# One substitution for all four head pairs: the triangular inverse of an RWKV-7 layer, one 32x32 block per partition

## The chip, the cores and the metric

The kernel runs on one core of a Trainium2 chip. The metric is the device time of one execution in microseconds. Line numbers are those of the kernel before the change; lines of the changed kernel stand only in the order and the diff, and are 1 less behind the changed function and 2 less behind the place that calls it.

## What is computed

One decoder layer on 2048 tokens of width 1024: an RMS norm, one wide projection, three branches (RWKV-7 time mixing with 8 heads of 64, sliding-window attention, cross-attention into 256 memory tokens), a projection of each branch under a gate, their sum, and an output projection. The change lies in the RWKV branch, whose state is computed token by token in the reference:

```python
def rwkv7_scan(r, w, k, v, a, b):
    def step(S, inp):
        r_t, w_t, k_t, v_t, a_t, b_t = inp
        sa = jnp.einsum('bhvk,bhk->bhv', S, a_t)
        S = S * w_t[:, :, None, :] + sa[..., None] * b_t[:, :, None, :] + v_t[..., None] * k_t[:, :, None, :]
        y = jnp.einsum('bhvk,bhk->bhv', S, r_t)
        return S, y
...
h = rms_norm(x, norm_g[l])
p = h @ w_in[l]
...
merged = (gates[:, :, 0] * (y_a @ w_proj_a[l]) + gates[:, :, 1] * (y_b @ w_proj_b[l])
          + gates[:, :, 2] * (y_c @ w_proj_c[l]))
x = x + (merged.astype(x.dtype) @ w_out[l]).astype(x.dtype)
```

The kernel computes it in chunks of 64 tokens. Within a chunk the tokens depend on each other through a unit triangular 64x64 matrix per head, and its inverse is needed before the chunk's state can be computed.

## The kernel before

The tokens are worked on in four blocks of 512 (the loop over `sb`). A block has 8 chunks, and the 8 heads are taken as 4 pairs. For a block, two streams of work are written out beside each other. `stream_r` is the RWKV branch: `rwkv_prep` for each pair (projections, decays, the products of a chunk), `rwkv_inverse` for the triangular matrices of two pairs, and once all four pairs are through, `rwkv_chain`, which carries the state through the 8 chunks and ends with the normalised output of each pair. `stream_f` is all the rest: cross-attention heads, the attention pairs, the merges of two branches (`merge`) and the gates. Each stream yields numbers, `paced` multiplies them by the factors of `PACE` (line 38), and `weave` lets the stream with the smaller sum go on. That gives the order in which instructions are written.

From this order a planner in the kernel (`steps` and `lay_out`, called by `order`) makes the final one. It goes through the program with its own costs per instruction and puts down, engine by engine, which ready instruction comes next by its rank; a tile's buffer has to be free first. So a change of the pools, the pacing or one function can move instructions everywhere. Each engine's instructions then stand in this order, and so do the DMAs of each queue: most are issued by SyncE, the loads of x's rows by ScalarE.

Matmuls of the projections are done in float32r with each operand as a high and a low part, so three matmuls of 512 columns per product (`gemm3`, lines 532 to 534). A weight tile `whl` holds both parts of four 128x128 blocks, 4 KB per partition, and serves 12 matmuls. There are `WR` = 7 of them. In the first block the parts are made from the raw weight (`wblock`, ScalarE L513, VectorE L514) and mostly kept in DRAM; later blocks load them (L509). Outputs go through two PSUM buffers named `mm`. The factors of a pair lie in tiles `big`, also 4 KB per partition, `BIG` = 6 of them: QE, QO, AB and BK for a pair in `rwkv_prep`, and Q and B of a chunk in the chain. AB of a pair stays until `rwkv_inverse` has put the inverse into it.

`rwkv_inverse` works on two pairs, 16 matrices of 64x64. Their diagonal 32x32 blocks, 64 of them, are stored to DRAM (`fn`, L843) and loaded so that one partition holds one block (L885). As there are 128 partitions, each block is loaded twice, and partition p and p+64 each compute half of the columns. A forward substitution of 31 steps, a multiply (L890) and an add (L891) on VectorE each, inverts them. The result goes out (L893, `fy`) and comes back with a block's rows on the partitions (L896), is transposed (L899), and two bursts of 32x32 matmuls (L911 and L919, with copies of the first one's output by L914 between) make the off-diagonal blocks. ScalarE puts them into AB (L904, L923), and SyncE stores AB (`put`, L756) to DRAM, from where the chain fetches it chunk by chunk (L942). The call for pairs 0 and 1 stands ahead of `rwkv_prep` of pairs 2 and 3.

At the end of a block the chain's outputs are transposed (L1032), scaled, gated and split into high and low parts (L1062, L1063), and `merge` projects them (L1315 empties the PSUM buffer, L1316 adds). In the middle of this, `x_scales` prepares the next block: it loads rows of x (L1357), ScalarE sums their squares (L1359), VectorE adds the halves (L1361), POOL makes the scale, VectorE spreads it (L570) and TensorE transposes it (L572).

Of the kernel before, what the change touches and what calls it, by code (L numbers as in the profile page):

```python
# [9 lines left out]
F32 = mybir.dt.float32  # L10
# [4 lines left out]
AF = mybir.ActivationFunctionType  # L15
ALU = mybir.AluOpType
# [3 lines left out]
T, D, M = 2048, 1024, 256  # L20
TB = 512
NG = 9
WR = 7
BIG = 6
NRT = 6
AT1, AT2 = 4, 8
SCRATCH = 1024
# [5 lines left out]
NC_ = TB // C  # L33
# [1 line left out]
DEC = 0.5 * math.exp(-0.5)  # L35


PACE = [[[1.2] * 20 + [0.8] * 20, [1.35] * 120] for _ in range(2)]


B_R, B_K, B_V, B_WA, B_ZA, B_Q, B_SK, B_SV, B_ZB, B_XQ, B_ZC, B_G = 0, 4, 8, 12, 13, 17, 21, 22, 23, 27, 31, 35
# [275 lines left out]
def build(tc, A, nsb=4):  # L317
    nc = tc.nc
    es = ExitStack()
    V, S, G, PE = nc.vector, nc.scalar, nc.gpsimd, nc.tensor  # L320
# [8 lines left out]
    rp = pool("rp", 1)  # L329
# [15 lines left out]
    def rw_ps():  # L345
        return ps.tile([128, 512], F32, name="rw", bufs=2)
# [145 lines left out]
    dp = pool("dp", 1, space=bass.MemoryType.DRAM)  # L492
# [382 lines left out]
    def rwkv_inverse(group, parks, fn, fy):  # L875

        n = len(group) * NC_
        halves = [(slice(b, b + 32), slice(b + 32, b + 64)) for b in (0, 64)]
        Nb = rp.tile([128, 32, 32], F32, name="km", bufs=2)
        B = rp.tile([128, 16, 32], F32, name="Yi")  # L880
        flat = B.rearrange("p a t -> p (a t)")
        G.memset(flat, 0.0)
        for j in range(2):
            own = slice(64 * j, 64 * j + 64)
            nc.sync.dma_start(Nb[own], fn.rearrange("q i c s t -> (q i c) s t"))  # L885
            G.memset(flat[own, j:j + 511:34], 1.0)
        for s in range(31):
            w, m = 31 - s, s // 2 + 1
            bc = rp.tile([128, 16, 32], F32, name="ibc", bufs=2)
            V.tensor_tensor(bc[:, :m, :w], Nb[:, s, s + 1:].unsqueeze(1).to_broadcast([128, m, w]), B[:, :m, s:s + 1].to_broadcast([128, m, w]), op=ALU.mult)  # L890
            V.tensor_tensor(B[:, :m, s + 1:], B[:, :m, s + 1:], bc[:, :m, :w], op=ALU.add)  # L891
        for j in range(2):
            nc.sync.dma_start(fy.rearrange("q i c (a j) t -> j (q i c) a t", j=2)[j], B[64 * j:64 * j + 64])  # L893
        Y = rp.tile([128, n, 32], F32, name="Yi")
        for q in range(4):
            nc.sync.dma_start(Y[32 * q:32 * q + 32], fy[q].rearrange("i c s t -> s (i c) t"))  # L896
        yield 27
        X = rp.tile([128, n, 32], F32, name="ibc", bufs=2)
        V.transpose(X.rearrange("p a b -> p (a b)"), Y.rearrange("p a b -> p (a b)"))  # L899
        for i, g in enumerate(group):  # L900
            for q in range(4):
                qs = slice(32 * q, 32 * q + 32)
                to = slice(32 * (q ^ g[0] // 2 * 2), 32 * (q ^ g[0] // 2 * 2) + 32)
                S.activation(g[1][to, :, 32 * (q % 2):32 * (q % 2) + 32], Y[qs, i * NC_:(i + 1) * NC_], AF.Copy)  # L904
        R = rp.tile([128, n, 32], F32, name="ibc", bufs=2)
        pr = rw_ps().rearrange("p (c t) -> p c t", t=32)
        ms = []
        for i, g in enumerate(group):
            for c in range(NC_):
                for u, l in halves:  # L910
                    ms.append(PE.matmul(pr[l, i * NC_ + c], g[1][u, c, 32:64], X[u, i * NC_ + c], start=True, stop=True))  # L911
        together(ms)
        for u, l in halves:
            V.tensor_copy(R[l], pr[l])  # L914
        po = rw_ps().rearrange("p (c t) -> p c t", t=32)
        ms = []
        for c in range(n):
            for u, l in halves:
                ms.append(PE.matmul(po[u, c], R[l, c], Y[l, c], start=True, stop=True))  # L919
        together(ms)  # L920
        for i, g in enumerate(group):
            for (u, l), (to, _) in zip(halves, halves[::-1] if g[0] > 1 else halves):
                S.activation(g[1][to, :, 32:64], po[u, i * NC_:(i + 1) * NC_], AF.Copy)  # L923
        for g in group:
            put(g[1], parks[1], g[0], 0)
        yield 4
# [458 lines left out]
    for i, _ in enumerate(mem_kv(mT)):  # L1385
        if i == AT1:
            rb = x_scales(0)
        if i == AT2:
            masks()
            hT = x_cols(0, rb)  # L1390
    for sb in range(nsb):
        wa = proj(B_WA, hT)
        low = shift(wa, B_WA, pcol("mu_wa"), dcol("omu_wa"), sb, "rr_")
        S.activation(low[EV], low[EV], AF.Tanh)

        lwla = [rp.tile([128, TB], F32R, name=f"lwla{i}") for i in range(2)]
        for t, h, o in zip(lwla, (EV, OD), (OD, EV)):
            S.activation(t[h], low[h], AF.Copy)
            V.tensor_tensor(t[o], low[h], t[h].bitcast(F32), op=ALU.subtract)
        yas = []  # L1400
        ya, yb, yc_ = ([], []), ([], []), ([], [])
        accs = []

        def stream_r():
            parks = park(sb)
            dk = xp.tile([128, 4, NC_], F32, name="dk", bufs=1)
            Pl = xp.tile([128, 4, NC_], F32, name="Pl", bufs=1)
            yts = []
            for p0 in (0, 2):
                group = []  # L1410
                fn, fy = (dp.tile([4, 2, NC_, 32, 32], F32, name=f"{n}{sb}_{p0}") for n in ("fn", "fy"))
                for p in (p0, p0 + 1):
                    yield from rwkv_prep(p, p - p0, parks, dk, Pl, fn, sb, hT, lwla, group)
                yield from rwkv_inverse(group, parks, fn, fy)
                yts += [g[2] for g in group]
            yield from rwkv_chain(parks, dk, Pl, hT, yts, yas)
            yield 0.412

        def stream_f():
            for h in range(4):  # L1420
                yield from cross_head(h, sb, hT, *yc_)
            if not sb:
                rope_tables(0)
            yield from swa_kv(sb, hT)
            yield 6.938
            for j in range(4):
                yield from weave(swa_pair(j, sb, hT, *yb), merge(2, *yc_, accs, hT, first=True, orange=(2 * j, 2 * j + 1)))
            yield from merge(1, *yb, accs, hT)
            for o in range(8):
                gates.append(gate(0, o, hT))  # L1430
                yield 5.908

        gates = []
        for _ in weave(*(paced(g, PACE[min(sb, 1)][i]) for i, g in enumerate((stream_r(), stream_f())))):
            pass
        for p in range(4):
            split_y(yas[p], *ya, "a", p, sb)
        rb = None
        if sb + 1 < nsb:
            rope_tables(sb + 1)  # L1440
            rb = x_scales(sb + 1)
        parts = []
        for o in range(8):
            for _ in merge(0, *ya, accs, hT, gates=gates, orange=(o,)):
                pass
            parts.append(split_acc(accs[o]))
        if rb is not None:
            hT = x_cols(sb + 1, rb)
        output(sb, *zip(*parts))
# [91 lines left out]
```

## Time and profile before

| | |
|---|---|
| three runs | 2147.26 us median, 2144.42 to 2148.93 |
| the profiled execution | 2148.25 us, span 2146.4 us |
| TensorE busy | 2129.0 us, 99% |
| weight loads (PEld) | 1754.6 us, 82% |
| VectorE | 1418.3 us, 66% |
| ScalarE | 805.7 us, 38% |
| DMA | 519.18 MB, 242 GB/s |

A share of the span says how long an engine had something to do. The profile also lists what each engine waited for, the chain of work that ended last, and the instructions in order of time.

### The profile page before, as it was taken

The page shows a single profiled execution, that of the slowest core. Times are in us where ns is not written, and L with a number is a line of the kernel's source. Part 1 is how long each engine was busy: PE and PEld are TensorE (multiplying, and loading weights), DVE is VectorE, ACT ScalarE, POOL GpSimd, SP SyncE. Part 2 cuts the span into 40 slices and gives each one's busy share as a digit, 9 for nine tenths or more (in the row PEclk, how much of TensorE's full clock was granted, in tenths as well). Part 3 has the DMA queues.
Part 4 walks back from the last instruction along what each step waited for, and adds up shares of the span by engine and source line. Part 5 has one row for each costly group of instructions (what it writes and reads, how often), then busy time and mean ns, then how long its engine had stood idle before and what let it go on. Part 6 is the DMA issues. An engine that isn't in the chain of part 4 may idle for free.

```text
span 2146.4 us, 37466 instructions
## 1 busy us (share of the span) xinstructions
PE 2129.0 (99%) x14260; PEld 1754.6 (82%) x14260; DVE 1418.3 (66%) x3234; ACT 805.7 (38%) x1703; POOL 138.5 (6%) x180
## 2 busy tenths in 40 slices
PE   9999999999999999999999999999999999999999
PEld 7888887878888888878788888887878888888787
DVE  7879888568477787455647778736455777873532
ACT  7655554336343343204423434410523334331220
POOL 2101000001001000001000000000100010000000
PEclk9999999999999999999999999999999999999999
DMA  9987888988866677686876657777776666768665
GB/s 337 356 280 266 271 290 282 341 288 269 296 207 193 182 219 229 198 298 207 283 255 207 193 175 224 230 224 261 248 254 217 204 201 200 230 188 268 218 205 182
DMA packets 308595, 519.18 MB, mean 242 GB/s; under 512 B 89280, under 2 KB 175552, under 8 KB 308416
## 3 DMA queue, kind: packets, MB, share of 16 engines
q1 hardware_dynamic: 292288, 487.42, 70.1%
q10 hardware_dynamic: 16128, 29.37, 4.2%
q8 instruction: 113, 1.85, 0.3%
q14 instruction: 66, 0.54, 0.1%
HBM read 378.80 MB, written 137.89 MB: 241 GB/s over the span
## 4 chain that ended last, share of the span: by engine, by line
PE 89%; DMA 4%; DVE 3%; ACT 2%; issue 1%; POOL 0%; SPq 0%; ACTq 0%; DVEq 0%; POOLq 0%
PE mm L532 22%; PE mm L534 22%; PE mm L533 22%; PE mm L1332 1%; PE mm L1334 1%; PE mm L1333 1%; DMA rt<-in_x 1%; PE rw L1014 1%; PE oo L1281 1%; PE rw L997 1%; PE rw L829 1%; PE rw L848 1%; DVE whl L514 1%; PE oo L829 1%; DMA raw<-in_w_in 0%
## 5 line engine op out<-in xcount | busy, mean ns | idle before, releaser
L532 PE MATMUL mm<-hH,whl 128*128 128x512 f32 x1888 | 745.2, 395 | 1.5 <-DVE carry L740 1.4
L533 PE MATMUL mm<-hL,whl 128*128 128x512 f32 x1888 | 743.3, 394 | 0.1
L534 PE MATMUL mm<-hH,whl 128*128 128x512 f32 x1888 | 741.7, 393 | 0.0
L532 PEld LDWEIGHTS mm<-hH,whl 128*128 128x128 f32 x1888 | 354.7, 188 | 73.0 <-ACT whl L513 1.8
L534 PEld LDWEIGHTS mm<-hH,whl 128*128 128x128 f32 x1888 | 354.7, 188 | 71.8
L533 PEld LDWEIGHTS mm<-hL,whl 128*128 128x128 f32 x1888 | 355.0, 188 | 70.4 <-DVE hL L1381 0.6
L513 ACT ACTIVATE whl<-raw 128x512 fp32r<-128x512 f32 x174 | 109.1, 629 | 184.8 <-PE mm L534 135.0
L514 DVE TENSOR_TENSOR whl<-raw,whl 128x512 fp32r<-128x512 f32 x174 | 120.1, 692 | 64.4 <-ACT whl L513 61.4
L532 PE MATMUL mm<-yh,whl 128*128 128x512 f32 x384 | 151.9, 396 | 3.7 <-DVE g L1315 2.1
L534 PE MATMUL mm<-yh,whl 128*128 128x512 f32 x384 | 151.4, 394 | 0.0
L533 PE MATMUL mm<-yl,whl 128*128 128x512 f32 x384 | 150.7, 392 | 0.0
L1300 ACT ACTIVATE gt<-mm 128x512 f32<-128x512 f32 x64 | 37.7, 590 | 178.7 <-PE mm L534 178.7
L532 PEld LDWEIGHTS mm<-yh,whl 128*128 128x128 f32 x384 | 72.5, 189 | 20.8 <-DVE g L1315 2.9
L533 PEld LDWEIGHTS mm<-yl,whl 128*128 128x128 f32 x384 | 72.5, 189 | 15.0 <-DVE yl L1063 0.2
L534 PEld LDWEIGHTS mm<-yh,whl 128*128 128x128 f32 x384 | 72.5, 189 | 15.1
L1315 DVE SCALAR_TENSOR_TENSOR gt<-gt,mm 128x512 f32<-128x512 f32 x32 | 22.0, 687 | 94.3 <-PE mm L534 93.9
L485 POOL TENSOR_SCALAR st<-st 128x4 f32<-128x4 f32 (+1 forms) x32 | 13.2, 413 | 1031.4 <-DVE st L1091 401.4
L1339 DVE SCALAR_TENSOR_TENSOR ya<-mm,ya 128x512 f32<-128x512 f32 x16 | 11.0, 690 | 97.7 <-PE mm L1334 97.7
L1249 ACT ACTIVATE g<-g,mxs,st 128x128 f32<-128x128 f32 x128 | 61.5, 483 | 27.9 <-DVE mxs L1242 27.9
L890 DVE TENSOR_TENSOR ibc<-km,Yi 128x126 f32<-128x126 f32 (+22 forms) x248 | 63.0, 254 | 7.6 <-DMA km<-fn 1.2
L891 DVE TENSOR_TENSOR Yi<-Yi,ibc 128x126 f32<-128x126 f32 (+22 forms) x248 | 62.7, 253 | 5.0
L489 POOL TENSOR_TENSOR st<-st,mhalf 128x8 f32<-128x8 f32 (+1 forms) x36 | 53.7, 1491 | 3.0
(1829 smaller groups left out, 3587.0 us busy)
## 6 DMA issues: line engine op xcount, KB each, us to landing
whl<-k SPq DMA_DIRECT2D x474, 512.0 KB, 4.0
k<-whl SPq DMA_DIRECT2D x162, 512.0 KB, 4.8
raw<-in_w_in SPq DMA_DIRECT2D x118, 256.0 KB, 4.1
fq<-big SPq DMA_DIRECT2D x64, 256.0 KB, 4.3
fb<-big SPq DMA_DIRECT2D x64, 256.0 KB, 4.2
big<-fq SPq DMA_DIRECT2D x32, 512.0 KB, 6.6
big<-fb SPq DMA_DIRECT2D x32, 512.0 KB, 5.6
ya<-in_x ACTq DMA_DIRECT2D x32, 256.0 KB, 4.8
```

The source lines that it names most:

```text
L489: G.tensor_tensor(out, out, mhalf[:, :n], op=ALU.pow)
L513: S.activation(w[:, 0], raw, AF.Copy)
L514: V.tensor_tensor(w[:, 1], raw, w[:, 0].bitcast(F32), op=ALU.subtract)
L532: PE.matmul(out, lh, rh, start=i == 0, stop=False)
L533: PE.matmul(out, lh, rl, start=False, stop=False)
L534: PE.matmul(out, ll, rh, start=False, stop=i == n - 1)
L829: m = PE.matmul(g[:, c], BK[h, c0 + c], Q[h, c0 + c], start=True, stop=True)
L890: V.tensor_tensor(bc[:, :m, :w], Nb[:, s, s + 1:].unsqueeze(1).to_broadcast([128, m, w]), B[:, :m, s:s + 1].to_broadcast([128, m, w]), op= ...
L891: V.tensor_tensor(B[:, :m, s + 1:], B[:, :m, s + 1:], bc[:, :m, :w], op=ALU.add)
L1249: S.activation(P_, P_, AF.Exp, scale=r2[:, b, i:i + 1], bias=mx[:, b, i:i + 1], accum_out=mx[:, b, 2 + i:3 + i])
L1300: S.activation(t, gp, AF.Tanh, scale=0.5)
L1315: V.scalar_tensor_tensor(g, g, 1.0, pp, op0=ALU.add, op1=ALU.mult)
```

## The change

`rwkv_inverse` is called once per block of tokens, behind `rwkv_prep` of all four pairs. It then has 128 diagonal blocks, one for each partition: they are loaded once, a step works on s+1 columns instead of s//2+1, and one store and one load (in four parts) replace two of each. The two bursts of matmuls have 64 instead of 32 matmuls and two PSUM buffers each, and the copies between them are four instead of two. The temporary `ibc` shrinks from 2 KB to 1 KB per partition (two buffers), `Yi` grows from 2 KB to 4 KB, X and R move to the tag `km`. As the ABs of four pairs stay until the inverse is there, `BIG` goes from 6 to 7, and `WR` from 7 to 6, tiles of the same size. The pacing of `stream_r` up to the chain goes from 20 yields at 1.2 to 18 at 1.4, in all four blocks.

```diff
-WR = 7
-BIG = 6
+WR = 6
+BIG = 7
...
-PACE = [[[1.2] * 20 + [0.8] * 20, [1.35] * 120] for _ in range(2)]
+PACE = [[[1.4] * 18 + [0.8] * 20, [1.35] * 120] for _ in range(2)]
...
-        B = rp.tile([128, 16, 32], F32, name="Yi")
+        B = rp.tile([128, 32, 32], F32, name="Yi")
...
-        for j in range(2):
-            own = slice(64 * j, 64 * j + 64)
-            nc.sync.dma_start(Nb[own], fn.rearrange("q i c s t -> (q i c) s t"))
-            G.memset(flat[own, j:j + 511:34], 1.0)
+        nc.sync.dma_start(Nb, fn.rearrange("q i c s t -> (q i c) s t"))
+        G.memset(flat[:, ::33], 1.0)
         for s in range(31):
-            w, m = 31 - s, s // 2 + 1
-            bc = rp.tile([128, 16, 32], F32, name="ibc", bufs=2)
-            V.tensor_tensor(bc[:, :m, :w], Nb[:, s, s + 1:].unsqueeze(1).to_broadcast([128, m, w]), B[:, :m, s:s + 1].to_broadcast([128, m, w]), op=ALU.mult)
-            V.tensor_tensor(B[:, :m, s + 1:], B[:, :m, s + 1:], bc[:, :m, :w], op=ALU.add)
-        for j in range(2):
-            nc.sync.dma_start(fy.rearrange("q i c (a j) t -> j (q i c) a t", j=2)[j], B[64 * j:64 * j + 64])
+            w, m = 31 - s, s + 1
+            bc = rp.tile([128, 256], F32, name="ibc", bufs=2)[:, :m * w].rearrange("p (a t) -> p a t", t=w)
+            V.tensor_tensor(bc, Nb[:, s, s + 1:].unsqueeze(1).to_broadcast([128, m, w]), B[:, :m, s:s + 1].to_broadcast([128, m, w]), op=ALU.mult)
+            V.tensor_tensor(B[:, :m, s + 1:], B[:, :m, s + 1:], bc, op=ALU.add)
+        nc.sync.dma_start(fy.rearrange("q i c s t -> (q i c) s t"), B)
...
-        yield 27
-        X = rp.tile([128, n, 32], F32, name="ibc", bufs=2)
-        V.transpose(X.rearrange("p a b -> p (a b)"), Y.rearrange("p a b -> p (a b)"))
+        yield 30
+        X = rp.tile([128, n, 32], F32, name="km", bufs=2)
+        for b in range(0, n, 16):
+            V.transpose(X[:, b:b + 16].rearrange("p a b -> p (a b)"), Y[:, b:b + 16].rearrange("p a b -> p (a b)"))
...
-        R = rp.tile([128, n, 32], F32, name="ibc", bufs=2)
-        pr = rw_ps().rearrange("p (c t) -> p c t", t=32)
+        R = rp.tile([128, n, 32], F32, name="km", bufs=2)
+        pr = [rw_ps().rearrange("p (c t) -> p c t", t=32) for _ in range(2)]
...
-        for u, l in halves:
-            V.tensor_copy(R[l], pr[l])
-        po = rw_ps().rearrange("p (c t) -> p c t", t=32)
+        for b in range(2):
+            for u, l in halves:
+                V.tensor_copy(R[l, 16 * b:16 * b + 16], pr[b][l])
+        po = [rw_ps().rearrange("p (c t) -> p c t", t=32) for _ in range(2)]
...
-            for p0 in (0, 2):
-                group = []
-                fn, fy = (dp.tile([4, 2, NC_, 32, 32], F32, name=f"{n}{sb}_{p0}") for n in ("fn", "fy"))
-                for p in (p0, p0 + 1):
-                    yield from rwkv_prep(p, p - p0, parks, dk, Pl, fn, sb, hT, lwla, group)
-                yield from rwkv_inverse(group, parks, fn, fy)
-                yts += [g[2] for g in group]
+            group = []
+            fn, fy = (dp.tile([4, 4, NC_, 32, 32], F32, name=f"{n}{sb}") for n in ("fn", "fy"))
+            for p in range(4):
+                yield from rwkv_prep(p, p, parks, dk, Pl, fn, sb, hT, lwla, group)
+            yield from rwkv_inverse(group, parks, fn, fy)
+            yts += [g[2] for g in group]
```

The planner then lays out everything anew. Three places of the new order bear on what follows. In the rows a name like `g_10628` is a buffer with its number.

VectorE at the boundary of the second and third block, where `x_scales` of the third block meets the first output tiles of `merge`. Before:

```order
L614 TENSOR_SCALAR cosT<-rt 128x512
L514 TENSOR_TENSOR whl<-raw,whl 128x512
L1361 TENSOR_TENSOR rs<-ss 128x4
L1315 SCALAR_TENSOR_TENSOR g_10628<-g_10628,mm 128x512
L514 TENSOR_TENSOR whl<-raw,whl 128x512
L1316 TENSOR_TENSOR mB<-mB,g_10628 128x512
L570 COPY rt<-rs 128x512
```

And now:

```order
L614 TENSOR_SCALAR cosT<-rt 128x512
L514 TENSOR_TENSOR whl<-raw,whl 128x512 x2
L1314 SCALAR_TENSOR_TENSOR g_10463<-g_10463,mm 128x512
L1315 TENSOR_TENSOR mB<-mB,g_10463 128x512
L1360 TENSOR_TENSOR rs<-ss 128x4
L1321 TENSOR_TENSOR mB<-mB,g_11001 128x512
L1314 SCALAR_TENSOR_TENSOR g_10558<-g_10558,mm 128x512
```

The instruction that empties the first `mm` buffer (L1315, now L1314) stood behind the sum `rs` and now stands ahead of it; that of the second output tile stays behind it.

SyncE's queue in the second block, the stores of AB (`fb`) behind the second burst and the chain's first fetch of them, among loads of weight tiles. Before:

```order
L756 DMA fb_0_6544<-big 128x4x128
L756 DMA fb_1_6545<-big 128x4x128
L509 DMA whl<-k_5085 128x1024
L509 DMA whl<-k_5092 128x1024
L756 DMA fb_0_6544<-big 128x4x128
L756 DMA fb_1_6545<-big 128x4x128
L509 DMA whl<-k_5140 128x1024
L942 DMA big<-fb_0_6544 128x1024
```

And now, the last five of eight stores and the fetch:

```order
L756 DMA fb_1_6431<-big 128x4x128
L509 DMA whl<-k_4963 128x1024
L756 DMA fb_0_6430<-big 128x4x128
L509 DMA whl<-k_4971 128x1024
L756 DMA fb_1_6431<-big 128x4x128
L509 DMA whl<-k_4978 128x1024
L756 DMA fb_0_6430<-big 128x4x128
L509 DMA whl<-k_5089 128x1024
L756 DMA fb_1_6431<-big 128x4x128
L509 DMA whl<-k_5097 128x1024
L941 DMA big<-fb_0_6430 128x1024
```

There were four stores ahead of the first fetch and are eight, and a weight load stands behind nearly each of them. On TensorE the order has 108 dense matmuls between the second burst and the chain's first use of AB (L1006) where it had 70 (109 and 71 in the first block).

TensorE at the end of the first block, from the last transposes of the chain's output (L1032, now L1031). Rows with `hH` and `hL` are matmuls of a gate, rows with `yh` and `yl` of the projection of that output. Before:

```order
L1032 MATMUL rw<-c_ident,rt 128x128 x4
L534 MATMUL mm<-hH,whl 128x512
L532 MATMUL mm<-hH,whl 128x512
L533 MATMUL mm<-hL,whl 128x512
L534 MATMUL mm<-hH,whl 128x512
L532 MATMUL mm<-hH,whl 128x512
L533 MATMUL mm<-hL,whl 128x512
L534 MATMUL mm<-hH,whl 128x512
L532 MATMUL mm<-hH,whl 128x512
L533 MATMUL mm<-hL,whl 128x512
```

And now:

```order
L1031 MATMUL rw<-c_ident,rt 128x128 x4
L534 MATMUL mm<-hH,whl 128x512
L532 MATMUL mm<-hH,whl 128x512
L533 MATMUL mm<-hL,whl 128x512
L534 MATMUL mm<-hH,whl 128x512
L532 MATMUL mm<-hH,whl 128x512
L533 MATMUL mm<-hL,whl 128x512
L534 MATMUL mm<-hH,whl 128x512
L532 MATMUL mm<-yh,whl 128x512
L533 MATMUL mm<-yl,whl 128x512
```

31 matmuls of gates stood between the last transposes and the projection; 7 do now. Of the projection, 9 matmuls of each of two output tiles come next, which need the first three pairs, and then those of the fourth.

## Rows read from the trace of the kernel before

**Rows 1.** The page, part 1: busy us of each engine, share, instructions.
```profile
PE 2129.0 (99%) x14260; PEld 1754.6 (82%) x14260; DVE 1418.3 (66%) x3234; ACT 805.7 (38%) x1703; POOL 138.5 (6%) x180
```

**Rows 2.** Windows: stretch, its length, each engine's busy us, PEclk, DMA share, GB/s.
```profile
200.00:300.00 100.00, 98.41 (x731) 81.76 (x730) 85.86 (x177) 51.19 (x107) 6.70 (x10) 1.00 0.84 273
...
600.00:700.00 100.00, 100.00 (x539) 83.46 (x538) 70.95 (x158) 39.44 (x85) 8.79 (x10) 1.00 0.67 201
...
1038.00:1042.00 4.00, 4.00 (x14) 3.23 (x13) 2.34 (x4) 1.23 (x2) 0.00 (x0) 0.57 0.97 321
```

**Rows 3.** What TensorE waited for: us in total, times, longest.
```profile
PE mm L532 <- DVE g L1315: 2.1, 1, 2.1
PE mm L532 <- DVE carry L740: 1.4, 1, 1.4
PE as__11203 L572 <- DVE rt L570: 1.2, 1, 1.2
PE mm L532 <- DVE gt L1315: 1.2, 1, 1.2
```

**Rows 4.** Timeline of TensorE around a second burst: start, us, instruction, idle before.
```profile
1282.67 0.39 PE L533 MATMUL mm<-hL,whl 128*128 128x512 f32 x1
1282.99 1.20 PE L919 MATMUL rw<-Yi,ibc 32*32 32x32 f32 x64
1284.12 0.50 PE L765 MATMUL rw<-lwla,whl 128*128 128x512 f32 x1
1284.46 0.40 PE L766 MATMUL rw<-lwla,whl 128*128 128x512 f32 x1
```

**Rows 5.** The substitution's multiply: the page's group, and one shape by form.
```profile
L890 DVE TENSOR_TENSOR ibc<-km,Yi 128x126 f32<-128x126 f32 (+22 forms) x248 | 63.0, 254 | 7.6 <-DMA km<-fn 1.2
...
L890 DVE TENSOR_TENSOR ibc<-km,Yi 128x126 f32<-128x126 f32 x24 | 7.0, 290 | 0.4
```

**Rows 6.** Timeline of TensorE at the boundary of the second and third block.
```profile
1029.45 0.39 PE L532 MATMUL mm<-yh,whl 128*128 128x512 f32 x1
...
1033.30 0.39 PE L534 MATMUL mm<-yh,whl 128*128 128x512 f32 x1
1035.83 0.50 PE L532 MATMUL mm<-yh,whl 128*128 128x512 f32 x1 [2.13 <-DVE g L1315]
...
1037.78 0.75 PE L572 MATMUL as__11203<-c_ident,rt 128*128 128x128 f32 x4 [1.22 <-DVE rt L570]
```

**Rows 7.** The chain that ended last in that stretch: start, us, what.
```profile
1025.95 8.22 DMA rt<-in_x
...
1035.01 0.07 DVE rs L1361
...
1035.09 0.68 DVE g L1315
```

**Rows 8.** SyncE's queue's waits (us, times, longest); landing times of weight tiles.
```profile
SPq L509 <- PE mm L534: 789.7, 352, 7.0
...
SPq L843 <- DVE big L836: 49.0, 14, 7.0
...
DMA to landing us min/median/max: 2.7/4.1/9.9
```

**Rows 9.** Timeline of VectorE between two bursts of the third block.
```profile
1280.66 0.68 DVE L914 COPY ibc<-rw 32x512 f32<-32x512 f32 x1
```

**Rows 10.** The page, part 6: DMA issues, KB each, median us to landing.
```profile
fb<-big SPq DMA_DIRECT2D x64, 256.0 KB, 4.2
...
big<-fb SPq DMA_DIRECT2D x32, 512.0 KB, 5.6
```

**Rows 11.** Timelines of TensorE, ScalarE and VectorE at the end of the first block.
```profile
497.84 0.60 PE L1032 MATMUL rw<-c_ident,rt 128*128 128x128 f32 x4
...
502.82 0.63 ACT L1062 ACTIVATE yh<-ya 128x512 fp32r<-128x512 f32 x1 [1.16 <-DVE ya L1040]
...
503.91 0.68 DVE L1063 TENSOR_TENSOR yl<-ya,yh 128x512 fp32r<-128x512 f32 x1
```

More of the change, by code (lines that the diff above doesn't have):

```diff
@@ L910, in rwkv_inverse @@
                 for u, l in halves:
-                    ms.append(PE.matmul(pr[l, i * NC_ + c], g[1][u, c, 32:64], X[u, i * NC_ + c], start=True, stop=True))
+                    ms.append(PE.matmul(pr[i // 2][l, i % 2 * NC_ + c], g[1][u, c, 32:64], X[u, i * NC_ + c], start=True, stop=True))
         together(ms)
-        for u, l in halves:
-            V.tensor_copy(R[l], pr[l])
-        po = rw_ps().rearrange("p (c t) -> p c t", t=32)
+        for b in range(2):
+            for u, l in halves:
+                V.tensor_copy(R[l, 16 * b:16 * b + 16], pr[b][l])
+        po = [rw_ps().rearrange("p (c t) -> p c t", t=32) for _ in range(2)]
         ms = []
@@ L918, in rwkv_inverse @@
             for u, l in halves:
-                ms.append(PE.matmul(po[u, c], R[l, c], Y[l, c], start=True, stop=True))
+                ms.append(PE.matmul(po[c // 16][u, c % 16], R[l, c], Y[l, c], start=True, stop=True))
         together(ms)
@@ L922, in rwkv_inverse @@
             for (u, l), (to, _) in zip(halves, halves[::-1] if g[0] > 1 else halves):
-                S.activation(g[1][to, :, 32:64], po[u, i * NC_:(i + 1) * NC_], AF.Copy)
+                S.activation(g[1][to, :, 32:64], po[i // 2][u, i % 2 * NC_:(i % 2 + 1) * NC_], AF.Copy)
         for g in group:
```

## The prediction

> **What bounds the kernel now.** I read the page's first part, then the windows, then the list of what TensorE waited for. TensorE is busy 2129.0 of 2146.4 us, and VectorE, the next engine, 1418.3 [rows 1]. That share alone could hide stalls, because the ends of matmuls are modelled, so I checked it by the weight loads (PEld). In a stretch without any TensorE idle time they fill 83.46 of 100 us [rows 2]. Over the whole span they fill 1754.6 us; divided by 0.8346 that is 2102 us of unbroken streaming. So at most 44 us of the span, 2%, is anything but streaming, and part of that is changes of the array's tile shape, which are work too. The list of waits agrees: the longest on VectorE's results are single ones of 2.1, 1.4, 1.2 and 1.2 us [rows 3]. A change that leaves TensorE's matmuls as they are can therefore move the end by those few microseconds, or by new waits, and by nothing else.
>
> The Trainium skill (Trainium Kernel Development and Optimization, Performance Expectations) says that matmul busy time flatters and that the share of weight loading is the better measure of the distance to the limit. By that rule alone 82% would leave 18% of the span open. The trace differs: a stretch without idle time stands at 83% as well.
>
> **The change part by part.**
>
> *TensorE.* The number of matmuls stays: two bursts of 64 for four pairs where there were twice two bursts of 32, in each of four blocks. The price of a burst is read where it stands alone [rows 4]. Dense matmuls start 0.227 us apart (17 steps from 1029.45 to 1033.30 [rows 6]). Before the burst 0.32 us pass (1282.67 to 1282.99), so 0.09 us for entering; the matmul behind it takes 0.34 us, so 0.11 us for returning. How much of the burst's own 1.13 us is its end, the rows don't part; I take 0.1, between 0 and 0.2. One burst fewer saves about 0.3 us. The order has 8 bursts fewer, 2.4 us. It also parts four second bursts from the chain's first burst, into which they ran before, and each now returns to dense work and leaves it again: 4 x 0.2 = 0.8 us back. Sum -1.6 us.
>
> *VectorE.* The substitution had 248 multiplies of 254 ns mean, 63.0 us, and as many adds of the same shapes [rows 5]. It now has 124 of each, with 176 elements on average (the sum of (31-s)(s+1) over 31 steps, divided by 31). A step of 126 elements took 290 ns; 176 elements cost between that and 290 x 176/126 = 405 ns. So 248 instructions cost 72 to 100 us instead of 126. All of that lies beside TensorE, which is busy through it, so the gain counts nothing by itself. The same is true of the halved DMAs of the round trip through memory.
>
> *The boundary of the second and third block.* This is the largest wait, and the order changes exactly there. TensorE stops at 1033.5 for 2.13 us, then again for 1.22 us [rows 6]. The chain shows why [rows 7]: a load of the next block's rows of x is issued at 1025.95 and lands 8.22 us later; ScalarE sums its squares; VectorE adds the sums (L1361) at 1035.01; and only behind that stands L1315, which empties the matmul's PSUM buffer at 1035.09. There are two such buffers, so TensorE runs dry. In the new order the first L1315 (now L1314) stands ahead of the sum. TensorE then has one more output tile to compute, 12 matmuls x 0.227 = 2.7 us, which covers the 2.13. The second wait, for the transposed scales, stays: its chain still begins at the landing. Behind the two waits the granted clock was 0.57 over 4 us [rows 2], so for most of that time at 1.2 instead of 2.4 GHz, which cost (1 - 0.57) x 4 = 1.7 us. The single wait of 1.4 us for L740 left the clock at 1.00 in its stretch, 200 to 300 us [rows 2], so I take the dip away with the first wait. Together -3.8 us; the bounds are 0 (the landing later still) and -5.1 (the second wait gone too).
>
> *VectorE late in the first block.* The waits for L740 (1.4) and for L1315 on gt (1.2) [rows 3] fall where VectorE splits fresh weights and does prep or substitution work. Half as many substitution steps, moved behind the fourth pair, thin this out, but the fourth pair now carries it all. I take half, -1.3 us, between -2.6 and +1.
>
> *One weight tile fewer.* A weight tile serves 12 matmuls, 2.7 us. With seven, a load is issued when a tile comes free and must have landed six tiles later, 16.3 us; with six, 13.6 us. Loads land in 4.1 us as a median and 9.9 at worst, and the sync queue does wait for tiles to come free, 352 times [rows 8], so the ring is always full and it is this lead that counts. The worst landing alone still fits. I charge nothing; what hides it is the 3.7 us left.
>
> *Between the two bursts.* Four copies of 0.7 us now stand between them instead of two [rows 9]. The order gives 13 dense matmuls, 3.0 us, instead of 11. The first two copies can start when half the burst is done. They need 2.1 to 3.1 us: between 0 and 0.3 us late, four times, so +0.5.
>
> *Handing over to the chain.* Eight stores of factors instead of four stand between the second burst and the chain's first fetch, 4.2 us to land and then 5.6 [rows 10]. The order puts about 108 dense matmuls (24.5 us) there instead of 70 (15.9). Behind the second burst the chain's first burst needs a PSUM buffer, and both are taken now. Cover is there for each; I charge 0, with +1.5 as the upper bound.
>
> *End of the first block.* The last transposes begin at 497.84; the halves of y that the projection needs are there at 503.45 and 504.59 [rows 11], so 5.6 and 6.75 us later. Now only 7 gate matmuls and 18 of the projection stand in between, 0.45 + 25 x 0.227 = 6.1 us. The first half fits, the second is used 0.5 us later and just misses. +0.5 us, between 0 and 1.5. Before, 31 gate matmuls covered it.
>
> *Sum.* -1.6 - 3.8 - 1.3 + 0.5 + 0.5 = -5.7 us. The profiled execution took 2148.25 us, 1.0 above the median of the three runs (2147.26), and holds the clock dip that another run may lack (they spread over 4.5 us). 2148.25 - 5.7 = 2142.5; against the median this is -0.22%.
>
> **The rivals.**
>
> *The wait moves on (no change).* The landing of x's rows stays as late as it was, and the second L1314 stands behind the sum. If the load lands 2 us later than in this profile, TensorE stops at the third output tile instead of the second and the dip comes too. Then only the bursts' 1.6 and the 1.3 remain, less 1.0: 2146.3. For it speaks that a load of weights can take 9.9 us [rows 8], 1.7 more than the 8.22 of this load; against it that one whole tile of cover is new. The Trainium skill (Trainium Kernel Development and Optimization, Key Constraints) says that DMAs of all queues share the same 16 engines and interleave; by that a shorter ring of loads on one queue frees nothing for x's rows on another, and the time would be the 2146.3. The trace agrees in that the DMA share was 0.97 in the window at 1038 [rows 2].
>
> *The ring runs dry (slower).* The sync queue runs in order. Its longest hold for a factor's masking was 7.0 us (L843) [rows 8]. If a hold of that length meets a landing of 9.9, the tile comes 16.9 us after its turn: 0.6 us late with seven tiles, 3.3 with six, and a clock dip of 1.7 with it, 5.0 us each time. Two such places cancel the gain and pass 0.2%; three give 2142.5 + 15 = 2157.5. Against it: holds of 7 us and landings of 9.9 are both the longest of hundreds, and no TensorE wait on a weight load is in [rows 3].
>
> *VectorE's time comes out at the end (it was the limit after all).* If TensorE had room and waited for VectorE all along, the 26 to 54 us less of VectorE work would show, some 40 of them: 2148 - 40 = 2108. The 83.46% of an unbroken stretch [rows 2] speaks against it, and so do waits of 6 us in all [rows 3]. The Trainium skill's rule on weight loading, named above, would make this likelier.
>
> **How the numbers follow.** The forecast gets 0.48, the wait that moves on 0.37, the dry ring 0.13, VectorE's time 0.02. A measurement of this kernel tells about 0.2% (4.3 us) from no change. Faster: 0.48 + 0.02 = 0.50; within 0.2%: 0.37; slower: 0.13. The forecast is 2142.5. Its low end adds the bounds: 1.3 more in the first block, 1.3 at the boundary, the 1.0 charged, and the 1.0 between median and profile: about 2137. The range reaches down to 2136, and up to 2152, which takes in the rival at 2146 with its unknown +1.5 and +1.5 and one dry place.
>
> **What would show it.** Right: the dense matmuls' counts unchanged, no TensorE wait above 1.5 us at the boundary of the second and third block, granted clock 1.00 there, VectorE's busy time 30 to 50 us less, idle TensorE time 12 us or less. Wrong: TensorE waits that end with a weight load or with L1314 behind the sum, more than one clock dip, a gap between the two bursts or before the chain's first use of the factors, or a wait for y at the end of a block.

## The result and the profile after

| | before | after |
|---|---|---|
| median of 11 runs each | 2147.49 us | 2156.3 us |
| range | 2144.23 to 2152.66 | 2152.65 to 2163.22 |
| profiled execution, span | 2148.25, 2146.4 | 2155.74, 2154.0 |
| TensorE, VectorE busy | 2129.0, 1418.3 | 2131.8, 1383.5 |

The ratio is 1.0042, 95% interval 1.0032 to 1.0051: 0.4% slower where 0.2% faster was forecast, and above the range. Lines are those of the changed kernel from here on, 1 or 2 less than before.

The page of the changed kernel, part 1, answers to [rows 1]:

```profile
span 2154.0 us, 37067 instructions
...
PE 2131.8 (99%) x14260; PEld 1753.7 (81%) x14260; DVE 1383.5 (64%) x2986; ACT 815.6 (38%) x1705; POOL 136.6 (6%) x164
```

TensorE does the same 14260 matmuls. VectorE has 34.8 us less to do, and the end came later all the same. The groups by line of the changed kernel show that the substitution cost what was worked out (84.3 us where [rows 5] gave 126, inside 72 to 100):

```profile
L889 DVE TENSOR_TENSOR Yi<-Yi,ibc 128x31 f32<-128x31 f32 (+15 forms) x124 | 42.2, 340 | 2.4
L888 DVE TENSOR_TENSOR ibc<-km,Yi 128x31 f32<-128x31 f32 (+15 forms) x124 | 42.1, 339 | 2.7 <-DMA km<-fn 0.3
```

TensorE's waits in the changed kernel (us in total, times, longest), to be read beside [rows 3]:

```profile
PE as__2010 L1186 <- ACT g L1182: 3.1, 1, 3.1
...
PE mm L1331 <- DVE g L1314: 2.1, 3, 1.1
...
PE rw L996 <- DMA Zt<-fv: 1.2, 2, 0.7
...
PE rw L1005 <- DMA big<-fb: 0.8, 2, 0.6
PE rw L918 <- issue: 0.7, 1, 0.7
```

The waits of before are gone: L740 and L1315 on `gt` in the first block, and the 2.1 us for L1315 at the boundary of the second and third block. Others have come. To see where the time is made I took the start of the first L829 matmul (the products of a chunk, in `rwkv_prep`) of each block, counted from the kernel's first matmul in both traces:

| stretch | before | after | difference |
|---|---|---|---|
| first block, up to L829 of the second | 610.2 | 619.4 | +9.2 |
| second block | 526.4 | 523.7 | -2.7 |
| third block | 522.8 | 522.7 | -0.1 |
| fourth block, to the last matmul | 480.4 | 481.5 | +1.1 |

The loss is made in the first block, and more than the 7.5 us between the two traces. Windows of the first block, before (TensorE busy, weight loads, VectorE, ScalarE, POOL, granted clock, DMA share, GB/s):

```profile
150.00:200.00 50.00, 50.00 (x242) 41.84 (x241) 47.70 (x123) 28.88 (x59) 6.82 (x8) 1.00 0.78 264
...
250.00:300.00 50.00, 48.41 (x326) 40.11 (x325) 46.43 (x85) 21.73 (x39) 2.88 (x3) 1.00 0.84 279
...
500.00:550.00 50.00, 49.48 (x219) 40.12 (x218) 47.28 (x82) 29.88 (x58) 3.64 (x3) 1.00 0.81 273
```

and after:

```profile
150.00:200.00 50.00, 46.94 (x210) 38.71 (x209) 41.24 (x79) 28.42 (x45) 5.73 (x7) 0.93 0.73 248
...
250.00:300.00 50.00, 50.00 (x320) 42.05 (x319) 40.13 (x84) 23.70 (x54) 3.72 (x4) 1.00 0.80 254
...
500.00:550.00 50.00, 45.63 (x203) 36.31 (x202) 38.49 (x68) 27.96 (x54) 5.06 (x4) 1.00 0.66 220
```

The stretch at 250 us gained the wait that the forecast named. The one at 150 us lost 3.1 us of TensorE and, at a granted clock of 0.93, another (1 - 0.93) x 50 = 3.5 us; the one at 500 us lost 3.9.

**At 177 us** ScalarE's queue of the changed kernel reads:

```profile
172.24 1.28 ACT L610 ACT_TABLE_LOAD   x1
...
174.80 1.28 ACT L781 ACT_TABLE_LOAD   x1
176.09 0.63 ACT L781 ACTIVATE rt<-rt 128x512 f32<-128x512 f32 x1
176.74 1.28 ACT L612 ACT_TABLE_LOAD   x1
178.04 0.63 ACT L612 ACTIVATE rt<-rt 128x512 f32<-128x512 f32 x1
...
179.09 0.58 ACT L1182 ACTIVATE g<-mm 128x512 f32<-128x512 f32 x1
```

The Exp of the third pair's prep (L781) has come between the two Sin of the rope tables (L610, L612), and each change of function loads a table, 1.28 us. L1182 waits behind them, and TensorE for it, 3.06 us. Behind that the granted clock was 0.50 for 6.8 us, from 180.8 to 187.6 us; dense matmuls started 0.43 us apart there instead of 0.227. A window inside it:

```profile
181.00:187.00 6.00, 6.00 (x20) 5.02 (x19) 5.27 (x13) 2.43 (x5) 0.73 (x1) 0.50 0.38 131
```

**At the end of the first block** TensorE waited 5.0 us between 480 and 590 us where it had waited 0.5 for L570. After:

```profile
PE mm L1331 <- DVE g L1314: 1.7, 2, 1.1
PE as__5808 L572 <- DVE rt L570: 1.5, 1, 1.5
PE mm L532 <- DVE g L1314: 1.2, 1, 1.2
PE mm L1331 <- DVE ya L1338: 0.4, 1, 0.4
PE as__6226 L1331 <- DVE ya L1338: 0.2, 1, 0.2
```

ScalarE's DMA queue shows what has moved. Before the change the loads of the next block's rows of x began 19 us ahead of the first output matmul (L1332 at 527.49):

```profile
508.28 1.99 ACTq L1357 DMA_DIRECT2D rt<-in_x  x3
```

and after it 13 us ahead (L1331 at 533.53), behind the output's first two copies (L1319):

```profile
520.49 0.63 ACT L1319 ACTIVATE g<-mB 128x512 fp32r<-128x512 f32 x1
520.50 1.30 ACTq L1356 DMA_DIRECT2D rt<-in_x  x3
...
536.28 0.33 ACTq L1356 DMA_DIRECT2D rt<-in_x  x1
```

VectorE's sum for the next block's scales, which had come 1.5 us ahead of the first output matmul, now comes 7.8 us behind it. Before and after:

```profile
525.96 0.15 DVE L1361 TENSOR_TENSOR rs<-ss 128x4 f32<-128x4 f32 x1
...
541.30 0.15 DVE L1360 TENSOR_TENSOR rs<-ss 128x4 f32<-128x4 f32 x1
```

So the next block's rope tables and scales, which were all but done by the time the output began, now reach into it, where VectorE also empties PSUM (L1314) and splits weights.

### The profile page after: what moved, and what is told of

Same layout as the page of the kernel before. It is cut to its first block, busy times and chain, and to the rows that moved or that the text cites. A ratio compares the mean times of both kernels' runs of the same rounds, so it can differ in the third digit from the quotient of the medians.

```text
span 2154.0 us, 37067 instructions
## 1 busy us (share of the span) xinstructions
PE 2131.8 (99%) x14260; PEld 1753.7 (81%) x14260; DVE 1383.5 (64%) x2986; ACT 815.6 (38%) x1705; POOL 136.6 (6%) x164
## 4 chain that ended last, share of the span: by engine, by line
PE 83%; DVE 7%; DMA 6%; ACT 2%; issue 1%; POOL 0%; SPq 0%; ACTq 0%; DVEq 0%
PE mm L533 21%; PE mm L534 20%; PE mm L532 20%; DVE Yi L889 1%; PE mm L1331 1%; PE mm L1333 1%; PE mm L1332 1%; DVE ibc L888 1%; DMA rt<-in_x 1%; PE rw L1013 1%; PE rw L829 1%; PE rw L996 1%; DMA Zt<-fv 1%; PE oo L1280 1%; PE rw L848 1%
## 5 line engine op out<-in xcount | busy, mean ns | idle before, releaser
L1314 DVE SCALAR_TENSOR_TENSOR gt<-gt,mm 128x512 f32<-128x512 f32 x32 | 22.0, 688 | 106.6 <-PE mm L534 98.9
L1331 PE MATMUL mm<-whl,g 128*128 128x512 f32 x128 | 50.2, 392 | 2.4 <-DVE g L1314 2.1
L1333 PE MATMUL mm<-whl,mB 128*128 128x512 f32 x128 | 49.8, 389 | 0.0
```

Of the source, the lines that this page charges most:

```text
L1314: V.scalar_tensor_tensor(g, g, 1.0, pp, op0=ALU.add, op1=ALU.mult)
L1331: PE.matmul(op[tt], mh[k][:, tk], wh, start=k == 0, stop=False)
L1333: PE.matmul(op[tt], ml[k][:, tk], wh, start=False, stop=k == 7)
```

## The experiments

"First" is the first block up to L829 of the second, "rest" what follows, each against the trace of before (610.2 and 1529.6 us); the ratio is of medians to runs of before on the same chip.

| run | ratio, 95% interval | first | rest |
|---|---|---|---|
| the change | 1.0042, 1.0032 to 1.0051 | +9.2 | -1.7 |
| e1_ring6 | 0.9991, 0.9982 to 1.0001 | +2.5 | -4.8 |
| e2_copy_ahead | 1.0037, 1.0023 to 1.0050 | +11.1 | -1.7 |
| e3_sooner_tail | 1.0212, 1.0196 to 1.0227 | +50.3 | -3.1 |
| e4_two_then_four | 0.9993, 0.9984 to 1.0002 | +1.1 | -2.6 |
| e5_preps_early | 1.0008, 0.9997 to 1.0018 | +2.2 | -0.2 |
| e6_chain_early | 1.0145, 1.0113 to 1.0176 | +32.0 | -2.9 |
| e7_all_early | 1.0136, 1.0108 to 1.0164 | +34.2 | -4.8 |
| e8_tables_early | 1.0006, 0.9998 to 1.0015 | +3.8 | -1.0 |
| e9_tables_early_pace14 | 1.0035, 1.0021 to 1.0048 | +10.6 | -3.1 |
| e10_before_tables_early | 1.0062, 1.0047 to 1.0078 | +11.5 | +1.0 |
| e11_four_repaced | 0.9984, 0.9975 to 0.9993 | +4.5 | -0.2 |
| e12_two_then_four_repaced | 0.9977, 0.9968 to 0.9987 | 0.0 | -6.3 |

The profiled execution of e11 was the slowest of its 12 (2152.64 against a median of 2147.23), so its two landmarks may be too high by a few us.

**The ring alone (e1_ring6).** Before, with

```diff
-WR = 7
+WR = 6
```

> The kernel before with six weight tiles instead of seven and nothing else; the planner lays it out anew. Theory A (the loss of 8.8 us was made at two places of the first block: ScalarE's queue at 177 us, 4.9 us, and the end of the block, 5.1 us): 2147.5 us as before, give or take 2 for the new order. Theory B (the shorter ring of weight tiles costs it, spread over the whole run): about 2156, most of the loss.

Measured 2146.58, no slower than before. Theory B falls. And the waits at the boundary of the second and third block went here too (rest -4.8): in this order, too, the first L1315 stands ahead of the sum `rs`. So they belonged to one order of VectorE's queue, and no change of the inverse is needed to lose them. The first block lost 2.5 us all the same: a new order alone can cost that much there.

**The copy moved ahead (e2_copy_ahead).** The changed kernel, in ScalarE's queue at 172 us only:

```diff
+L781 ACTIVATE rt<-rt
 L610 ACT_TABLE_LOAD
 L610 ACTIVATE rt<-rt
 L513 ACTIVATE whl<-raw
 L779 ACTIVATE Pl<-Pt
-L781 ACTIVATE rt<-rt
+L1182 ACTIVATE g<-mm
 L612 ACTIVATE rt<-rt
 L513 ACTIVATE whl<-raw
-L1182 ACTIVATE g<-mm
```

> The changed kernel with two instructions moved in ScalarE's queue near 177 us: the prep's Exp (L781) ahead of the first Sin (L610), and the copy out of PSUM (L1182) ahead of the second Sin (L612); no other order changes. Theory A: TensorE's wait of 3.1 us for that copy and the stretch at granted clock 0.50 behind it go, 3.2 + 1.7 = 4.9 us: 2156.3 - 4.9 = 2151.4; if the clock dips all the same, 2153. Theory B (ring) and theory C (the single inverse costs a little in each block, between the chain's start and its first use of the factors): 2156, the wait filled by something else.

Measured 2157.47. The wait did go: set against the changed kernel matmul by matmul (TensorE's order is the same), this run was 5.1 us ahead from 188 to 200 us: the wait, and 2.7 us by the clock, gained matmul by matmul over the 6.8 us at 0.50. It then gave all of it back. TensorE's waits of this run between 170 and 420 us:

```profile
PE rw L829 <- DVE big L818: 1.6, 1, 1.6
PE rw L918 <- issue: 1.5, 1, 1.5
PE rw L1005 <- DMA big<-fb: 1.3, 1, 1.3
PE oo L1280 <- DVE g L1268: 0.8, 1, 0.8
```

Behind the first two of these waits the clock fell as well:

```profile
200.00:203.00 3.00, 3.00 (x13) 2.39 (x11) 2.79 (x6) 0.82 (x2) 2.46 (x2) 0.50 0.47 173
391.00:394.00 3.00, 3.00 (x34) 2.25 (x34) 1.12 (x2) 2.25 (x5) 0.40 (x2) 0.50 0.90 271
```

L829 is the third pair's burst, and VectorE had come only 2 us ahead: it is busy nearly without a gap there. That took 3.7 of the 5.1 us back by 205 us; L918, the second burst, took 2.3 at 390 us, where no instruction of VectorE is shown as the cause. So the wait at 177 us, though real, was worth nothing by itself. Theory A falls in its first half.

**The tail sooner (e3_sooner_tail).**

```diff
-PACE = [[[1.4] * 18 + [0.8] * 20, [1.35] * 120] for _ in range(2)]
+PACE = [[n, [1.35] * 120] for n in ([1.4] * 10 + [1.3] * 8 + [0.8] * 20, [1.4] * 18 + [0.8] * 20)]
```

> The changed kernel with the pacing of the first block's RWKV stream at 1.3 instead of 1.4 from its 11th yield on: the chain starts some 8 us sooner in the weave, and the loads of the next block's rows of x again stand ahead of the output's copies (L1319) in ScalarE's queue. Theory A: the waits between 513 and 561 us, 5.1 us more than before the change, go; the one at 177 us stays: 2156.3 - 5.1 = 2151.2. Theory B and C: 2156, as the ring and the single inverse are as they were.

Measured 2194.43. Its two longest waits are for the inverse itself:

```profile
PE rw L1005 <- DMA big<-fb: 12.8, 3, 12.1
PE rw L909 <- DVE km L897: 7.7, 1, 7.7
```

Between 480 and 640 us only 1.2 us of waits were left, instead of 5.0, so the end of the block did come clean. But the chain can't start sooner than the inverse is there: even with TensorE waiting, 88 us lay between the fourth pair's last masks (L836 at 280.3) and the first burst (368.7). The prediction had not asked how much slack the inverse has in the first block. In the changed kernel the transposes (L897) end at 377.3 and the first burst starts at 380.1: less than 3 us.

**Two pairs at a time in the first block only (e4_two_then_four).**

```diff
+            for ps in ((0, 1), (2, 3)) if not sb else ((0, 1, 2, 3),):
...
+                yield from (rwkv_inverse if sb else rwkv_inverse_2)(group, parks, fn, fy)
```

(`rwkv_inverse_2` is the function of before; the first block is paced as before.)

> The first block inverts two pairs at a time with the pacing of before, the other three all four pairs at once with the pacing of the change; six weight tiles, seven factor tiles. Theory A: the first block is as before the change and the other blocks keep what the change gained there (2.7 us by the landmarks of the two traces: 3.7 in the second block, 0.1 in the third, 1.1 lost in the fourth): 2147.5 - 2.7 = 2144.8. Theory B: 2156. Theory C: three quarters of the loss stays, 2147.5 + 6.6 = 2154.

Measured 2147.48, ratio 0.9993. The loss is the first block's: theories B and C fall. The later blocks were to give 2.7 us; by the table above it is 1.7 (the second block's 3.7 counted only up to its output), and here the trace shows 2.6 in the rest, 1.5 in all.

**Preps early (e5_preps_early).**

```diff
+PACE = [[n, [1.35] * 120] for n in ([1.2] * 16 + [2.2] * 2 + [0.8] * 20, [1.4] * 18 + [0.8] * 20)]
```

> The changed kernel with the first block paced so that the preps of the four pairs come at 1.2 as before the change and the inverse gets the rest (2.2 for its two yields); the chain starts where it did (16 yields of 133.2 at 1.2 and 34 at 2.2 are 234.6, against 234.1). Theory D (in the first block VectorE is the bound in stretches, and the pacing at 1.4 puts the third pair's prep on top of the first rope tables and leaves the single substitution a short window): the waits near 177 to 200 and at the hand-over near 387 and 414 us go, about 5 us, and the end of the block stays late: 2156.3 - 5 = 2151. Theory A' (what costs at 177 is only ScalarE's queue, as moved in the run before, and the rest follows the planner's chance): no better than 2156.

Measured 2150.69. The path of the inverse in the first block, by the first and last start of each operation: the fourth pair's last masks (L836), the first burst, the chain's first use. Before the change (there the last two pairs):

```profile
L836 DVE TENSOR_TENSOR big<-yps,big x2: 673/673/673, 260.0 to 295.4; 64x512 f32<-64x512 f32 x2
...
L911 PE MATMUL rw<-ibc,big x64: 191/191/212, 389.0 to 390.0; 32*32 32x32 f32 x64
...
L1006 PE MATMUL rw<-W,big x48: 218/218/267, 411.4 to 422.3; 64*64 64x64 f32 x48
```

After the change:

```profile
L836 DVE TENSOR_TENSOR big<-oo,big x2: 693/693/693, 206.7 to 282.7; 64x512 f32<-64x512 f32 x2
...
L909 PE MATMUL rw<-km,big x128: 191/191/212, 380.1 to 382.1; 32*32 32x32 f32 x128
...
L1005 PE MATMUL rw<-W,big x48: 218/218/267, 416.7 to 428.2; 64*64 64x64 f32 x48
```

In this run:

```profile
L836 DVE TENSOR_TENSOR big<-oo,big x2: 690/690/690, 189.9 to 248.6; 64x512 f32<-64x512 f32 x2
...
L909 PE MATMUL rw<-km,big x128: 191/191/212, 342.1 to 344.1; 32*32 32x32 f32 x128
...
L1005 PE MATMUL rw<-W,big x104: 218/218/268, 377.4 to 430.0; 64*64 64x64 f32 x104
```

From the last mask to the first burst it took 93.6 us before, 97.4 after and 93.5 here: the substitution for four pairs got about the same window as that for two. From there to the chain's first use it took 22.4 us before and 36.6 after (35.3 here), with bursts twice as long and eight stores instead of four. That is the order's choice and not what the hand-over needs: in e3, where TensorE waits for it, it took 22.8 us (368.7 to 391.5). Nor does it make the chain late. Counted in the traces, 2520 matmuls stand ahead of the chain's first use on TensorE where 2517 did, so the bursts stand sooner and the chain stands where it stood; that it starts 5.3 us later (416.7 against 411.4) is the sum of the waits and the clock ahead of it. In this run everything is 34 to 39 us sooner, the rows of x are loaded from 488.83 us on, and 0.8 us of waiting is left at the end of the block. A wait remains at 182 us, with a clock of 0.50 for 3.4 us behind it:

```profile
PE as__2022 L572 <- DVE rt L570: 2.7, 1, 2.7
```

It is the stretch of the wait at 177 us again: VectorE was busy 30.42 of the 31 us around it with rope tables, the third prep and the split of weights. So theory D's 2151 was met by luck: the wait that it said would go is still there, and the end of the block, which it left late, is what came clean.

**Chain early (e6_chain_early, e7_all_early).** As e5 with

```diff
+[1.2] * 16 + [1.9] * 2 + [0.8] * 20
```

in the first block, and in e7 the pacing of e5 in the later three.

> As the run with the preps early, with the inverse's two yields at 1.9, so that the chain and the end of the RWKV stream come some 10 us sooner in the weave. Theory D: the inverse still has 34 x 1.9 = 65 us where the changed kernel gives it 34 x 1.4 = 48 and the run with the sooner tail 34 x 1.3 = 44, so it isn't waited for, and the loads of the next block's rows stand ahead of the output's copies again: the first block loses nothing, 2156.3 - 9.2 = 2147. Theory E (any earlier chain waits for the single inverse, as in the run with the sooner tail, as the substitution can only begin behind the fourth pair): a wait of 5 us or more for the transposes (L897) or the fetched factors (L1005), 2160 or more.

> As the run with the chain early in the first block, and the three later blocks paced with the preps at 1.2 and the inverse at 2.2. Theory D: the first block as in that run; in the later blocks, where no weights are split, VectorE has room and the pacing of the preps matters little: within 3 us of that run. Theory E: 2160 or more, from the first block.

Measured 2180.22 and 2177.99: theory E. The inverse is as early as in e5, but the chain's first use stands 104 matmuls sooner in TensorE's order. In e6 TensorE waited 7.0 us for the factors (L1005) and then did the chain's steps with nothing between them:

```profile
370.00:400.00 30.00, 16.75 (x336) 14.71 (x336) 13.24 (x40) 1.09 (x2) 0.00 (x0) 0.56 0.71 247
```

Why the planner had no dense matmuls for those 30 us was not tried. e7 adds one thing: with the new pacing its later blocks took 4.8 us less than before, as they did in e1 with the inverse and the pacing of before.

**The tables elsewhere (e8, e9, e10).** The first rope tables two cross-attention heads sooner, on e5, on the change and on the kernel before:

```diff
             for h in range(4):
+                if (h, sb) == (2, 0):
+                    rope_tables(0)
                 yield from cross_head(h, sb, hT, *yc_)
-            if not sb:
-                rope_tables(0)
```

> As the run with the preps early (2.2 for the inverse in the first block), with the first rope tables written two cross-attention heads sooner, ahead of the third head instead of behind the fourth. Theory D (VectorE, without a gap from 161 to 192 us there, has the tables, the third pair's prep and the split of weights at once): the wait of 2.7 us for L570 at 182 us and the dip of the clock behind it (0.96 over 40 us, 1.6 us) go: 2150.7 - 4.3 = 2146.4. Theory F (the wait moves on to the next place, as in the run with the copy moved ahead): 2150.7, with a new wait of 2 us or more in the 60 us behind it.

> The changed kernel, pacing as it is, with the first rope tables two cross-attention heads sooner. Theory D: the wait of 3.1 us near 177 us and its dip go, 4.9 us, and the waits at the end of the first block (5.1 us) and at the hand-over stay, as they come from the late chain: 2156.3 - 4.9 = 2151.4. Theory F: 2156 to 2157, as in the run with the copy moved ahead.

> The kernel before with the first rope tables two cross-attention heads sooner. Theory D: there the tables met the substitution of the first two pairs, which can be put off, and TensorE waited for nothing between 150 and 250 us, so nothing is gained: 2148, give or take 2 for the new order. If it gains over 4 us, the tables' place and not the single inverse is what the changed kernel lost by.

Measured 2150.52, 2156.46 and 2161.71: the times of theory F in e8 and e9, and a loss in e10. In e8 the wait moved to L740 at 150 us (3.3 us), ahead of its old place and not behind it as F had said. In e9 no wait above 1 us is left between the kernel's start and 400 us, and the end of the block takes the gain back, with a clock of 0.50 for 6.8 us behind it; now the chain's own output is late:

```profile
PE mm L532 <- ACT yh L1061: 2.5, 1, 2.5
PE mm L1331 <- DVE ya L1338: 2.2, 1, 2.2
PE rw L1031 <- DVE rt L1028: 1.9, 1, 1.9
```

e10 missed my expectation by 13 us. It waits 3.2 us for L740 at 150 us, and at 266 us, where VectorE does the third pair's masks ahead of the instruction that empties PSUM (L1049 of the kernel before):

```profile
PE mm L532 <- DVE g L1049: 5.7, 1, 5.7
```

So the kernel before, too, loses over 11 us in its first block when VectorE's work there changes places, without any change of the inverse. And the boundary of the second and third block kept its order here, and its waits (1.56 and 1.22 us). In the kernel before, the substitution of the first two pairs had been 15.7 us of work spread over 164 to 210 us, and TensorE waited for nothing there. That it is work that can be put off is argued from the order (its burst comes at 232 us) and not tested.

**Repaced (e11_four_repaced, e12_two_then_four_repaced).** All blocks of the change paced as e5's first; and e4 with its later blocks so paced.

```diff
+[1.2] * 16 + [2.2] * 2 + [0.8] * 20
```

> The changed kernel with all four blocks paced with the preps at 1.2 and the inverse at 2.2. If waits add up block by block (theory G), the first block is that of the run with the preps early (2.2 us more than before the change by its landmarks) and the later ones those of the run with all blocks early (from 34.2 to 29.4, 4.8 us less): 2148.5 + 2.2 - 4.8 = 2145.9, and the single inverse costs nothing once it has its window. Theory H (a gain in one block is taken back by a wait in the next): 2150.6, as in the run with the preps early.

> Two pairs at a time in the first block as before the change, four at once in the later three, these paced with the preps at 1.2 and the inverse at 2.2. Theory G: the first block of the run with two then four (1.1 us more than before) and the later ones of the run with all blocks early (4.8 us less): 2148.5 + 1.1 - 4.8 = 2144.8, faster than both kernels. Theory H: 2147.5, as in the run with two then four.

Measured 2147.23 (ratio 0.9984) and 2144.54 (0.9977): theory G by the times, and both are a little faster than the kernel before. The trace of e11 doesn't show the 4.8 us in the later blocks (rest -0.2). e12 does (rest -6.3), but e1 had -4.8 there without the change, so by these two traces at most 1.5 us of it can be put down to the single inverse and its pacing. e12, the fastest of all, has no single wait above 1.3 us but the one at the kernel's start:

```profile
span 2140.5 us, 37165 instructions
...
PE 2124.8 (99%) x14260; PEld 1752.6 (82%) x14260; DVE 1391.4 (65%) x3048; ACT 807.0 (38%) x1703; POOL 139.0 (6%) x168
...
PE mm L532 <- DVE carry L740: 1.3, 1, 1.3
```

## Why the prediction was wrong

The reading that nothing but TensorE's waits counts was right, if the clock behind them is counted too: 34.8 us less of VectorE gave nothing by themselves. So was the boundary of the second and third block: the granted clock is 1.00 from 1030 to 1050 us, and up to its output the second block is 3.7 us shorter, where 3.8 was said. The near hit is partly luck, as both waits are gone, also the second, which the forecast kept; with it 5.1 us should have come. The order of VectorE's queue did it, as was said; e1 and e10 show that it was the luck of a new order and not the inverse's doing. The weight tile costs nothing (e1), as said. The copies between the bursts cost 0.7 us once (L918), where 0.5 was said, and the hand-over 0.6 us in the first block (L1005), inside its bounds.

The 1.6 us for fewer bursts are not to be seen. TensorE's idle time over the whole span grew by 4.7 us and the time lost by the clock by 1.7, which is 6.4 of the 7.5 us between the traces; about 1 us more was left where 1.6 less was said.

Besides this term two steps failed, both in the first block.

*VectorE late in the first block*, put at -1.3, between -2.6 and +1. The two waits did go, the full -2.6. But "half as many substitution steps thin this out" looked only at the places that had waited before. With the substitution of the first two pairs gone from there, the third pair's prep moved up to the rope tables and the weight splits (its first masks, L836, from 257 to 203 us), and TensorE ran into that: 3.1 us of waiting and, with 6.8 us at a clock of 0.50, 2.7 (matmul by matmul against e2) to 3.4 us ((1 - 0.50) x 6.8) of clock. Net +3.2 to +3.9. e2, e8 and e9 show that it can't be had back at one place.

*End of the first block*, put at +0.5, up to 1.5. I counted 25 matmuls of cover for the halves of y and forgot what else had been done under the 31 gate matmuls: the next block's tables, loads and scales. On TensorE the last transposes now stand behind 3437 matmuls instead of 3413, that is behind the 24 gate matmuls that had followed them. That cost 4.5 us (5.0 of waits against 0.5). In the two runs with an earlier tail, e3 and e5, only 1.2 and 0.8 us of waits are left there. In e5 this, not the wait at 177 us, is most of what brings the first block from +9.2 to +2.2. Why the planner put the gates first is not shown.

Of +9.2 this explains -2.6 + 3.1 + 2.7 to 3.4 + 4.5 + 0.7 (L918) + 0.6 (L1005), 9.0 to 9.7. The sum over all waits agrees: TensorE's idle time in the first block grew from 6.3 to 12.5 us, and the clock took up to 3.4. So it is shown where the time went, and e4 shows that it is the first block's. How much of it any new order would have cost is open: without the single inverse e1 lost 2.5 us there and e10 11.5. None of the rivals was it: the dry ring was the slower one, and no new wait for a weight load came. (The low end of the range adds up to 2137.9 and not 2137; nothing hangs on it.)

## What to carry to other kernels

When a long dependent piece is taken out of one place and put behind another, look at what moves into the place that it leaves: here the substitution shrank from 125.7 to 84.3 us, and the first block still lost 9 us, in part because other work of VectorE met where it had been. Then price every stretch where the second-busiest engine is full, in the block that has the most extra work, and not only the place of the largest old wait: in such a stretch one wait removed can turn up again elsewhere, in e2 some 20 us later, in e9 at the end of the block. And a cover counted in matmuls covers everything that used to lie under it, so list that first. Last, measure what a new order alone does before a gain or a loss of this size is put down to the change.

## What the runs showed of the hardware

A switch between Sin and Exp cost a table load of 1.28 us on ScalarE each time, three within 6 us where the two were interleaved. In the changed kernel the granted clock fell to 0.50 (the level of 1.2 GHz) for 6.8 us behind the wait of 3.06 us. The length of a single wait didn't decide it: in e2 the clock was 0.50 from 200 to 203 and from 391 to 394 us behind waits of 1.59 and 1.52 us, but behind waits of 1.07 and 1.51 us at the end of the changed kernel's first block it was 1.00, from 533 to 565 us. In e6 it was 0.56 over 30 us of chain steps with nothing between them, so that chain cost twice: by its gaps and by the clock.
